# Gate and up rows 4 to 21 by 20 products for 24 in groups of three rows, left sums on GpSimd, results kept in DRAM

## The chip, the cores and the metric

The kernel runs on one core of a Trainium2 chip. The metric is the device time of one execution in microseconds (us). Before the change it is 1108.66 us, the median of 3 runs (1106.58 to 1109.56). Lower is better.

Engines are named as in the profile: PE (TensorE, matrix products), PEld (its weight loads), DVE (VectorE), ACT (ScalarE), POOL (GpSimd) and SP (SyncE, which here only issues transfers). X<-Y means that an instruction writes X from Y.

## The reference

One step of a decoder layer on 544 tokens (512 of a prompt and 32 samples), width 1024, in fp32: half a feed-forward network, a mixer (attention beside an mLSTM), and half a feed-forward network again. The change touches both feed-forward halves alone:

```python
def half_ffn(x, g_pre, g_post, w_gate, w_up, w_down):     # w_gate, w_up: 1024 x 2816; w_down: 2816 x 1024
    h = rmsnorm(x, g_pre)
    u = jax.nn.silu(h @ w_gate) * (h @ w_up)
    return x + 0.5 * rmsnorm(u @ w_down, g_post)
```

## The kernel before

**Split numbers.** Every factor of a product is split into a high part (a cast to fp32r) and a low part (the factor less its high part). A product is three matmuls: high by high, high by low, low by high. `parts` (L240) makes the two: a cast on ACT (L241), then a subtraction on DVE (L242), whose two inputs both lie in SBUF.

**Tiles.** Tokens are columns (544, two halves of 272). 2816 hidden units are 22 rows of 128, and the contraction over 1024 is 8 tiles of 128. One matmul is 128 x 128 by 128 x 272.

**Gate and up rows 0 to 3** (`PLAIN`) are computed plainly (L588 to L595), row by row, by `mm3`. Rows 2 and 3 make eight jobs of 24 matmuls, while the right-hand factors for what follows are begun.

**Gate and up rows 4 to 21** are nine steps of two rows (`quadrants`, L488). A step takes [gate; up] x two halves of the contraction x two halves of the tokens by 7 products in place of 8. Sums of weight blocks (left sums) and sums of token blocks (right sums, made once in `right_parts` and `factors`) feed the products; both are made on DVE (`plus`, L499, and `less`/`neither`, L454/L457). A product is 24 matmuls (`seven`), a step 168. Results come out of PSUM through copies on ACT (L531) and additions on DVE (L499 with a PSUM input), then silu (L535, L541) and a multiplication (L544, L549). Weights of the next step are loaded one step ahead, 1024 KB each for gate and up, on SP's queue. The kept hidden rows 0 to 15 stay in SBUF (`ha`; rows 0 to 3 make a trip through DRAM, `u_keep`), and rows 16 to 21 (`OWN`) are split into high and low parts at once.

**Down** (`down`, L703) begins with a lead: plain products of rows 16 to 21, 12 groups of 18 matmuls, for which only those rows are needed. Under the lead, the first factors of the kept rows 0 to 15 are made (`making`), for 7 products of four quarters each. Weights of the down product come in on SP's queue and are added up by accumulating transfers on POOL's queue (L732).

**The order of work.** Each engine runs its own queue in order. A list scheduler writes the queues from the program: it may move an instruction ahead of others on its engine when it thinks it ready, and a buffer is handed to its next tile when the last reader of the old one is done. Split weights go through `w_tiles` (L244), three buffers of each kind; PSUM has eight banks (`acc` 3, `aux` 3, `smp` 2).

Of the kernel before, what the change touches and what calls it, by code (L numbers as in the profile page):

```python
# [50 lines left out]
PRODUCTS = (1, 5, 6, 2, 7, 3, 4)  # L51
# [138 lines left out]
class _Halves:  # L190
# [4 lines left out]
    def __getitem__(self, key):  # L195
        p, k, *c = key
        if isinstance(k, slice):
            a, b = k.indices(KT)[:2]
            assert a // WK == (b - 1) // WK
            k, i = slice(a % WK, a % WK + b - a), a // WK  # L200
        else:
            k, i = k % WK, k // WK
        return self.tiles[i][(p, k, *c)]


class _Builder:
# [213 lines left out]
    def u_tiles(self, li, ctx):  # L420

        return ctx.enter_context(self.tc.tile_pool(name="u%d" % li, bufs=1))


    def right_parts(self, gi, place, pool):

        nc = self.nc
        n = place[:, 0:KT]

        def scaled(k0):  # L430
            for k in range(k0, k0 + WK):
                nc.vector.scalar_tensor_tensor(out=n[:, k, :], in0=self.X[:, k, :],
                                               scalar=self.minus[:, gi * KT + k:gi * KT + k + 1], in1=self.r,
                                               op0=ALU.mult, op1=ALU.mult)
        scaled(0)
        yield
        h8 = self.h8, "h8"
        places = {p: [(pool, "t")] if p in (1, 5, 6) else [h8] for p in PRODUCTS}
        quarters = [tuple(n[:, k:k + WK, c:c + HALF] for k in (0, WK) for c in (0, HALF))]
        making = self.factors(places, quarters, PRODUCTS)  # L440
        for _ in range(2):
            next(making)
            yield
        scaled(WK)
        yield from making
# [42 lines left out]
    def quadrants(self, loaded, raws, small, kept, put, beside, making):  # L488

        nc = self.nc
        flat = self.X.tiles[0].rearrange("p k t -> p (k t)")
        s3 = flat[:, 0:1024].rearrange("p (k m) -> p k m", k=WK)
        space = flat[:, 1024:1024 + 2 * T].rearrange("p (a t) -> p a t", a=2)
        C0, C1 = slice(0, HALF), slice(HALF, T)

        def plus(out, x, y):
            nc.vector.tensor_tensor(out=out, in0=x, in1=y, op=ALU.add)  # L499
        for u in range(PLAIN, KF, 2):  # L500
            (g0, g1), (u0, u1) = ((r[:, 0:WK], r[:, WK:KT]) for r in loaded)
            if PLAIN < u < KF - 2:
                loaded = raws(u + 2)
            uu = kept(u) if u < KEEP else space
            p1, p5, u2 = (small.tile([128, 2, HALF], F32, name=name) for name in ("p1", "p5", "u2"))
            a, b = [], []
            for p in PRODUCTS:
                if u == PLAIN:
                    next(making, None)
                    if p == 5:  # L510
                        loaded = raws(u + 2)

                if p == 5:
                    plus(s3, g0, u0)
                    plus(u0, u0, u1)
                elif p == 6:
                    plus(u0, u0, g0)
                elif p == 3:
                    plus(u0, u0, g1)
                src = {1: g0, 2: g1, 4: u1, 7: s3}.get(p, u0)  # L520
                w = [x.rearrange("p (k a) m -> p k (a m)", a=2) for x in self.w_tiles()]
                self.parts(src, *w)
                for r in range(2):
                    if p == 1:
                        a.append(self.acc.tile([128, 512], F32, name="acc")[:, 0:HALF])
                    elif p == 5:
                        b.append(self.ps_tile()[:, 0:HALF])
                    ps = b[r] if p in (5, 3) else self.smp.tile([128, 512], F32, name="smp")[:, 0:HALF] if p == 2 else a[r]
                    self.seven(ps, p, w, slice(r * 128, r * 128 + 128), p in (1, 5, 2), p in (2, 3, 4))
                    if p in (1, 5, 6):  # L530
                        nc.scalar.copy(out={1: p1, 5: p5, 6: u2}[p][:, r], in_=ps)  # L531
                    elif p == 2:
                        x = uu[:, r, C0]
                        plus(x, ps, p1[:, r])
                        nc.scalar.activation(out=x, in_=x, func=AF.Silu, scale=-1.0)  # L535
                    elif p == 7:
                        plus(uu[:, r, C1], ps, p5[:, r])
                    elif p == 3:
                        x = u2[:, r]
                        plus(x, ps, x)  # L540
                        nc.scalar.activation(out=x, in_=x, func=AF.Silu, scale=-1.0)  # L541
                    elif p == 4:
                        x = uu[:, r, C0]
                        nc.vector.tensor_tensor(out=x, in0=ps, in1=x, op=ALU.mult)  # L544
                    if u == PLAIN:
                        next(beside, None)
                if p == 3:
                    x = uu[:, :, C1]
                    nc.vector.tensor_tensor(out=x, in0=x, in1=u2, op=ALU.mult)  # L549
            if u >= KEEP:  # L550
                put(u, uu)

    def ffn(self, li, hs, ws, gpre, gpost, finish, before=None, u=None, lead=None, done=None):
# [7 lines left out]
        with ExitStack() as ctx:  # L561
# [3 lines left out]
            spill = tc.dram_tile([128, PLAIN, T], F32, name="u_keep%d" % li)  # L565
# [78 lines left out]
            place = own.tile([128, 2 * OWN, T], F32, name="u")  # L644
            making = self.right_parts(gpre, place, factors)
# [4 lines left out]
            def raws(m):  # L650
                if m == PLAIN:
                    g = place[:, KT:2 * OWN].rearrange("p k t -> p (k t)")[:, 0:2048].rearrange("p (k m) -> p k m", k=KT)
                else:
                    g = self.raw.tile([128, 8, 256], F32, name="raw")
                u = self.X.tiles[1].rearrange("p k t -> p (k t)")[:, 0:2048].rearrange("p (k m) -> p k m", k=KT)
                if (m - PLAIN) % 4 == 0:
                    u = small.tile([128, 8, 256], F32, name="rawx")
                for r, w in zip((g, u), views):
                    nc.sync.dma_start(out=r, in_=w[:, :, m * 128:m * 128 + 256])
                return g, u  # L660


            steps = 3
            jobs = [(f, m, half) for m in range(2, PLAIN) for half in range(2) for f in (gate, upper)]
            ahead, last = 2, len(jobs) - 3
            done, w = 0, None
            for i, (f, m, half) in enumerate(jobs[:last]):
                if i % 4 == 0:
                    w = {gate: weight(), upper: weight()}
                if i == 0:  # L670
                    first = raws(PLAIN)
                f(m, half, w[f])
                upto = max(0, steps * (i + 1 - ahead) // (last - ahead))
                for _ in range(done, upto):
                    next(making)
                done = upto

            def beside():
                for f, m, half in jobs[last:]:
                    f(m, half, w[f])  # L680
                    yield
            ns = []

            def kept(m):
                if not ns:
                    ns.extend(self.ha.tile([128, WK, T], F32, name="ha") for _ in range(KEEP // WK))
                elif m == PLAIN + 2:
                    nc.gpsimd.dma_start(out=ns[0], in_=spill)
                return ns[m // WK][:, m % WK:m % WK + 2, :]

            def put(m, uu):
                i = 2 * (m - KEEP)
                if i == 0:
                    self.own = own.tile([128, 2 * OWN, T], F32R, name="u")
                s = self.own[:, i:i + 4].rearrange("p (a b) t -> p a b t", a=2)
                self.parts(uu, s[:, 0], s[:, 1])
                rows.update({m + a: (s[:, 0, a, :], s[:, 1, a, :]) for a in range(2)})
            self.quadrants(first, raws, small, kept, put, beside(), making)
            more.__exit__(None, None, None)
            self.down(li, ns, rows, factors, ctx.enter_context(tc.tile_pool(name="late%d" % li, bufs=2)), xd, gpost,  # L700
                      finish)

    def down(self, li, ns, rows, factors, late, xd, gpost, finish):  # L703
# [4 lines left out]
        t, h8 = (factors, "t"), (self.h8, "h8")  # L708
# [50 lines left out]
        def close():  # L759
            i, up, hs, w, ps = held.pop(0)  # L760
            for half, p in zip(hs, ps):
                plain(p, w, half, OWN - 2, 2, False, True)
                nc.scalar.activation(out=y[half][:, 4 * up + i, :], in_=p, func=AF.Copy, scale=-1.0 if up else 1.0)
        for i, up, hs in lead:
# [4 lines left out]
            for half, p in zip(hs, ps):  # L769
                plain(p, w, half, 0, OWN - 2, True, False)  # L770
# [1240 lines left out]
```

## Time and profile before

| | before |
|---|---|
| median of 3 runs | 1108.66 us (1106.58 to 1109.56) |
| profiled execution, first to last instruction | 1109.2 us |
| PE busy | 1088.8 us (98%), clock 0.995 |
| DVE busy | 855.4 us (77%) |
| ACT busy | 639.5 us (58%) |
| POOL busy | 163.2 us (15%), most of it issuing transfers |
| HBM | 144 GB/s over the span |

How to read it: a busy time is the time in which an engine had an instruction in execution, of the profiled execution's span. A wait is named after what ended it. The profile gives no time of the execution outside its span; that span lies 0.5 us above the median of the runs.

### The profile page before, as it was taken

The page shows a single profiled execution, that of the slowest core. Times are in us where ns is not written, and L with a number is a line of the kernel's source. Part 1 is how long each engine was busy: PE and PEld are TensorE (multiplying, and loading weights), DVE is VectorE, ACT ScalarE, POOL GpSimd, SP SyncE. Part 2 cuts the span into 40 slices and gives each one's busy share as a digit, 9 for nine tenths or more (in the row PEclk, how much of TensorE's full clock was granted, in tenths as well). Part 3 has the DMA queues.
Part 4 walks back from the last instruction along what each step waited for, and adds up shares of the span by engine and source line. Part 5 has one row for each costly group of instructions (what it writes and reads, how often), then busy time and mean ns, then how long its engine had stood idle before and what let it go on. Part 6 is the DMA issues. An engine that isn't in the chain of part 4 may idle for free. (4 is left out here: it accounts for less than half of the span.)

```text
span 1109.2 us, 21539 instructions
## 1 busy us (share of the span) xinstructions
PE 1088.8 (98%) x8610; PEld 1050.2 (95%) x8610; DVE 855.4 (77%) x1626; ACT 639.5 (58%) x1288; POOL 163.2 (15%) x212
## 2 busy tenths in 40 slices
PE   9999999999999999999999999999999999999997
PEld 8999999999999998899789888999999999999997
DVE  5898787887677898668666477799978778957865
ACT  6554544565567756666545466675555455555664
POOL 3100000001210424320333442001000000012000
PEclk9999999999999999999999999999999999999999
DMA  9723233237994346533345545864223323299832
GB/s 265 252 94 114 81 111 115 76 96 208 223 245 128 93 121 172 175 112 82 103 148 160 178 136 177 248 216 161 89 87 105 114 77 106 67 270 206 191 97 81
DMA packets 145588, 160.33 MB, mean 145 GB/s; under 512 B 6013, under 2 KB 135397, under 8 KB 144208
## 3 DMA queue, kind: packets, MB, share of 16 engines
q1 hardware_dynamic: 115008, 99.05, 29.5%
q0 software_dynamic: 27472, 57.14, 20.8%
q10 hardware_dynamic: 3008, 2.78, 0.9%
q8 instruction: 67, 1.10, 0.4%
q14 instruction: 33, 0.27, 0.1%
HBM read 143.19 MB, written 16.28 MB: 144 GB/s over the span
## 5 line engine op out<-in xcount | busy, mean ns | idle before, releaser
L241 ACT CAST wh<-raw 128x512 fp32r<-128x512 f32 (+2 forms) x165 | 126.8, 795 | 97.3 <-PE acc L254 34.3
L242 DVE TENSOR_TENSOR wl<-raw,wh 128x512 fp32r<-128x512 f32 (+2 forms) x165 | 146.9, 904 | 43.4 <-ACT wh L241 42.7
L253 PE MATMUL acc<-h,wh 128*128 128x272 f32 x552 | 165.7, 300 | 0.0
L255 PE MATMUL acc<-h,wl 128*128 128x272 f32 x552 | 161.4, 293 | 0.0
L254 PE MATMUL acc<-h,wh 128*128 128x272 f32 x552 | 161.0, 292 | 0.0
L483 PE MATMUL acc<-t,wh 128*128 128x272 f32 x472 | 136.7, 290 | 0.0
L485 PE MATMUL acc<-t,wl 128*128 128x272 f32 x472 | 136.5, 290 | 0.0
L484 PE MATMUL acc<-t,wh 128*128 128x272 f32 x472 | 136.1, 289 | 0.0
L253 PEld LDWEIGHTS acc<-h,wh 128*128 128x128 f32 x552 | 104.9, 190 | 8.1 <-issue 7.5
L255 PEld LDWEIGHTS acc<-h,wl 128*128 128x128 f32 x552 | 104.9, 190 | 0.6 <-issue 0.4
L254 PEld LDWEIGHTS acc<-h,wh 128*128 128x128 f32 x552 | 105.1, 190 | 0.3 <-DVE y L1459 0.2
L483 PE MATMUL acc<-h,wh 128*128 128x272 f32 x360 | 104.2, 290 | 0.0
L485 PE MATMUL acc<-h,wl 128*128 128x272 f32 x360 | 104.2, 289 | 0.0
L484 PE MATMUL acc<-h,wh 128*128 128x272 f32 x360 | 103.6, 288 | 0.0
L242 DVE TENSOR_TENSOR wl<-X,wh 128x1024 fp32r<-128x1024 f32 x66 | 80.7, 1223 | 28.3 <-ACT wh L241 28.3
L241 ACT CAST wh<-X 128x1024 fp32r<-128x1024 f32 x66 | 69.3, 1050 | 40.6 <-PE aux L484 26.0
L484 PEld LDWEIGHTS acc<-t,wh 128*128 128x128 f32 x472 | 89.0, 189 | 0.0
L483 PEld LDWEIGHTS acc<-t,wh 128*128 128x128 f32 x472 | 88.8, 188 | 0.0
L485 PEld LDWEIGHTS acc<-t,wl 128*128 128x128 f32 x472 | 88.7, 188 | 0.1
L732 POOL DMA_DIRECT2D late<-in_ffn_w_down_dram x12 | 18.8, 1563 | 439.4 <-DVE wl L242 241.6
L485 PE MATMUL aux<-h,wl 128*128 128x272 f32 x240 | 69.6, 290 | 0.4 <-DVE wl L242 0.4
L483 PE MATMUL aux<-h,wh 128*128 128x272 f32 x240 | 69.4, 289 | 0.0
(522 smaller groups left out, 3288.6 us busy)
## 6 DMA issues: line engine op xcount, KB each, us to landing
raw<-in_ffn_w_gate_dram SPq DMA_DIRECT2D x18, 1024.0 KB, 5.8
raw<-in_w_in_dram SPq DMA_DIRECT2D x28, 512.0 KB, 4.8
late<-in_ffn_w_down_dram POOLq DMA_DIRECT2D x12, 1024.0 KB
rawx<-in_ffn_w_up_dram SPq DMA_DIRECT2D x10, 1024.0 KB
X<-in_ffn_w_up_dram SPq DMA_DIRECT2D x8, 1024.0 KB, 5.4
raw<-in_ffn_w_down_dram SPq DMA_DIRECT2D x8, 1024.0 KB, 8.6
raw<-in_ffn_w_down_dram SPq DMA_DIRECT2D x10, 768.0 KB, 4.5
raw<-in_w_out_dram SPq DMA_DIRECT2D x7, 1024.0 KB, 5.3
```

Source lines behind the costliest of these rows:

```text
L241: self.nc.scalar.copy(out=high, in_=src)
L242: self.nc.vector.tensor_tensor(out=low, in0=src, in1=high.bitcast(F32), op=ALU.subtract)
L253: nc.tensor.matmul(ps, lhsT=wh, rhs=xh(k0 + k), start=st, stop=False)
L254: nc.tensor.matmul(ps, lhsT=wh, rhs=xl(k0 + k), start=False, stop=False)
L255: self.last_mm = nc.tensor.matmul(ps, lhsT=wl, rhs=xh(k0 + k), start=False, stop=sp).ins
L483: nc.tensor.matmul(ps, lhsT=wh[:, k, cs], rhs=high, start=st, stop=False, skip_group_check=True)
L484: nc.tensor.matmul(ps, lhsT=wh[:, k, cs], rhs=low, start=False, stop=False, skip_group_check=True)
L485: self.last_mm = nc.tensor.matmul(ps, lhsT=wl[:, k, cs], rhs=high, start=False, stop=sp, skip_group_check=True).ins
L732: nc.gpsimd.dma_start(out=ts[j], in_=rows_of(a, j, up), accum_op=ALU.add)
```

## The change

Rows 4 to 21 become six groups of three rows (`triples`, in place of `quadrants`). A group takes three rows x four blocks of contraction x two halves of tokens by 20 products in place of 24. A left block is 128 rows of gate and the same of up by two contraction tiles (128 x 512 in SBUF), a right block two contraction tiles by 272 tokens (128 x 544). A product is 12 matmuls, 6 for gate and 6 for up, so a group has 240.

- Left sums (`SUMS`, 16 in a group) run on POOL, in place of DVE, partly in the weight buffers themselves and partly in six scratch pieces s0 to s5 at the ends of these buffers.
- Right factors: 8 scalings on DVE as before, then 20 products' factors of 128 x 544, of which 16 need a sum, on POOL. They lie in the token tiles X0 and X1, which are free by then, and other pools. Two steps of this are taken after each of seven jobs, the rest in the first group. The jobs now all stand before the first group; before, three of them ran beside the first step.
- Every product's 128 x 512 left block is split by ACT and DVE as before; two products share one pair of split buffers.
- Products accumulate in eight chains (`CHAINS`), each with two PSUM banks, four at a time. Nine times in a group a chain's state in between is copied out by ACT for gate and up; seven times DVE adds PSUM to SBUF; seven further sums of 128 x 544 (`both`) run four on POOL and three on DVE.
- Weights are loaded in 8 transfers of 384 KB a group on SP's queue, into eight home buffers: four from `small` and `raw`, four from the kernel's `ha` tiles.
- So hidden rows 4 to 15 are no longer kept in `ha`: each half row is stored to DRAM by SP (136 KB each), and after the last group rows 0 to 15 are loaded back into four `ha` tiles by four transfers of 1088 KB on POOL's queue, where before one such transfer brought back rows 0 to 3. Rows 16 to 21 are split into `t` tiles.

The queues, as built. On POOL, inside rows 4 to 21 (`u`, `ha`, `raw`, `rawx` are home buffers, scratch pieces and places of results), before:

```order
L586 DMA u_keep_410<-sqe 128x272 x4
L688 DMA ha<-u_keep_410 128x2176
L732 DMA late_3000<-in_ffn_w_down_dram 128x8x256
L732 DMA late_3002<-in_ffn_w_down_dram 128x8x256
L732 DMA late_3000<-in_ffn_w_down_dram 128x8x256
```

and now, a third of the way through (L534 a left sum, L549 a sum of results):

```order
L549 TENSOR_TENSOR u_921<-u_921,ha_912 128x544
L549 TENSOR_TENSOR ha_911<-ha_911,u_921 128x544
L534 TENSOR_TENSOR raw_899<-raw_900,rawx2_897 128x512
L534 TENSOR_TENSOR ha_910<-raw_899,raw_900 128x512
L534 TENSOR_TENSOR rawx2_897<-rawx2_897 128x4x128
L534 TENSOR_TENSOR raw_899<-raw_899,rawx2_897 128x512
L534 TENSOR_TENSOR ha_909<-raw_900,raw_899 128x512
L534 TENSOR_TENSOR raw_900<-raw_900 128x4x128
L534 TENSOR_TENSOR rawx0_898<-raw_899,rawx0_898 128x512
L534 TENSOR_TENSOR ha_909<-ha_909 128x4x128
L549 TENSOR_TENSOR u_922<-u_922,ha_912 128x544
L549 TENSOR_TENSOR u_921<-u_921 128x544
```

POOL went from transfers alone to 20 sums a group.

On DVE, in the middle of rows 4 to 21, before (L499 a left sum or an addition out of PSUM):

```order
L499 TENSOR_TENSOR rawx<-rawx,raw 128x1024
L242 TENSOR_TENSOR wl<-rawx,wh 128x1024
L242 TENSOR_TENSOR wl<-raw,wh 128x1024
L499 TENSOR_TENSOR rawx<-rawx,raw 128x1024
L242 TENSOR_TENSOR wl<-X_85,wh 128x1024
L499 TENSOR_TENSOR X_85<-raw,X_86 128x1024
L499 TENSOR_TENSOR X_86<-X_86 128x1024
L499 TENSOR_TENSOR ha<-smp,p_1362 128x272
```

and now (L594 an addition out of PSUM, L792 the multiplication by the gate):

```order
L263 TENSOR_TENSOR wl_1489<-ha_909,wh_1488 128x512
L594 TENSOR_TENSOR ha_912<-acc_1371,ha_912 128x272
L263 TENSOR_TENSOR wl_1489<-ha_911,wh_1488 128x512
L594 TENSOR_TENSOR ha_912<-acc_1372,ha_912 128x272
L263 TENSOR_TENSOR wl_1524<-ha_911,wh_1523 128x512
L263 TENSOR_TENSOR wl_1524<-raw_899,wh_1523 128x512
L263 TENSOR_TENSOR wl_1563<-ha_909,wh_1562 128x512
L549 TENSOR_TENSOR ha_911<-ha_911,u_921 128x544
L263 TENSOR_TENSOR wl_1563<-ha_909,wh_1562 128x512
L594 TENSOR_TENSOR u_922<-aux_1391,ha_911 128x272
L594 TENSOR_TENSOR u_922<-aux_1392,ha_911 128x272
L792 TENSOR_TENSOR u_922<-u_922 128x272
```

The left sums of 128 x 1024 have left this queue; the subtractions are half as long and twice as many for the same weights.

On DVE at the passage to `down`, now (`ha` with 128x4x272 are sums of reloaded rows, raw_3374 the down weights of the lead):

```order
L263 TENSOR_TENSOR wl_3469<-raw_3374,wh_3468 128x768
L263 TENSOR_TENSOR u_3413<-ha_3357,u_3413 128x1088
L263 TENSOR_TENSOR t_3075<-u_922,t_3075 128x272
L496 TENSOR_TENSOR ha_3357<-ha_3357 128x4x272
L496 TENSOR_TENSOR ha_3356<-ha_3358,ha_3356 128x4x272
L496 TENSOR_TENSOR ha_3357<-ha_3359,ha_3357 128x4x272
L263 TENSOR_TENSOR wl_3513<-raw_3374,wh_3512 128x768
```

Before, the rows at this place read tiles that had been in SBUF; now three sums of reloaded tiles (the last two loaded are ha_3358 and ha_3359) stand ahead of the fourth split of the lead's weights.

The diff, cut to its core:

```diff
-PRODUCTS = (1, 5, 6, 2, 7, 3, 4)
+ROWS = 3
+ORDER = (11, 5, 4, 2, 1, 16, 7, 9, 8, 19, 0, 12, 17, 18, 6, 10, 13, 3, 14, 15)
+CHAINS = ((11, 4), (5, 7, 9), (2, 16, 0), (1, 8), (19, 12, 17), (18,), (6, 13, 14), (10, 3, 15))
+RIGHT = {11: ("00", 1, "21"), 5: ("00",), 4: ("00", 1, "31"), 2: ("21",), 1: ("20", -1, "21"), 16: ("10", 1, "21"),
...
+SUMS = {11: ("02=02-22", "s3=00-02"), 5: ("s0=10-13", "s0=s0-s3"), 4: ("10=10-20", "s1=13-10"),
+        2: ("s2=11-12", "s5=s2+s3"), 16: ("s2=s2+22",), 7: ("12=12-22",), 19: ("s4=01-03", "s2=s4-s2"),
+        0: ("s4=21-s4",), 18: ("s1=s1+s4", "s1=23-s1"), 3: ("01=01-21",)}
...
+        for i, p in enumerate(ORDER):
...
+                    nc.gpsimd.tensor_tensor(out=out, in0=x, in1=block(y), op=ALU.add if sign > 0 else ALU.subtract)
+                    x = out
+                self.parts(x, high, low)
+            yield
...
+    def left_sum(self, text, views):
...
+        self.nc.gpsimd.tensor_tensor(out=out, in0=x, in1=y, op=ALU.add if op == "+" else ALU.subtract)
...
+            for s, p in enumerate(ORDER):
+                if i == 0:
+                    next(making, None)
+                for text in SUMS.get(p, ()):
+                    self.left_sum(text, views)
+                if s % 2 == 0:
+                    wh, wl = (x.rearrange("p (b k a m) -> p b k a m", b=2, k=2, a=2) for x in
+                              (y.rearrange("p k m -> p (k m)") for y in self.w_tiles()))
+                self.parts(views[LEFT[p]], wh[:, s % 2], wl[:, s % 2])
...
+                if p == 1:
+                    both(at["8"], at["8"], at["1"], nc.gpsimd)
+                    both(at["11"], at["11"], at["10"], nc.gpsimd)
+                elif p == 16:
+                    both(at["8"], at["8"], at["9"])
...
+                for k in (2, 0, 3, 1):
+                    for a in range(2):
+                        c = (PLAIN + i * ROWS) * 128
+                        nc.sync.dma_start(out=homes[i % 2][k][:, :, a, :], in_=views[a][:, 2 * k:2 * k + 2, c:c + ROWS * 128])
...
+                if i:
+                    _take(making, 2)
...
+                if m < KEEP:
+                    nc.vector.tensor_tensor(out=x, in0=x, in1=g, op=ALU.mult)
+                    nc.sync.dma_start(out=spill[:, m, self.cols(half)], in_=x)
...
+            ns = [self.ha.tile([128, WK, T], F32, name="ha") for _ in range(KEEP // WK)]
+            for i, x in enumerate(ns):
+                nc.gpsimd.dma_start(out=x, in_=spill[:, WK * i:WK * i + WK])
```

More of the change, by code (lines that the diff above doesn't have):

```diff
@@ L203, in __getitem__, with __init__, one @@
         return self.tiles[i][(p, k, *c)]
+class _Pair:
+    def __init__(self, *tiles):
+        self.tiles = tiles
+    def one(self, a):
+        return self.tiles[a] if len(self.tiles) == 2 else self.tiles[0][:, a * HALF:a * HALF + HALF]
 class _Builder:
@@ L642, in ffn @@
             factors = ctx.enter_context(tc.tile_pool(name="t%d" % li, bufs=3))
-            place = own.tile([128, 2 * OWN, T], F32, name="u")
-            making = self.right_parts(gpre, place, factors)
+            making = self.right_parts(gpre, own, factors)
             more = tc.tile_pool(name="more%d" % li, bufs=1)
@@ L648, in ffn @@
             views = self.ffn_views(li)
[L650 to L660, printed above, removed]
@@ new lines, in places @@
+            def places(i):
+                if not spots:
+                    for _ in range(2):
+                        x = generic(own, (WK, T), name="u")
+                        spots.extend(x[:, j * T:j * T + T] for j in range(4))
+                names = ("8", "10", "11", "1", "9", "20", "01", "6", "y")
+                rest = iter(spots)
+                at = {}
+                for name in names:
+                    if name in ("8", "10"):
+                        flat = pieces[4 + 2 + (name == "10")][:, 6 * 256:6 * 256 + T]
+                    elif i == 0 and name in ("11", "1", "9"):
+                        t = "sq" if name == "11" else "sqe"
+                        at[name] = _Pair(*(self.tmp.tile([128, HA], F32, name=t, bufs=3 if t == "sq" else 4) for _ in range(2)))
+                        continue
+                    else:
+                        flat = next(rest)
+                    at[name] = _Pair(flat)
+                at["x"], at["21"] = at["1"], at["9"]
+                return at
@@ L664, in ffn @@
+            spots = []
             jobs = [(f, m, half) for m in range(2, PLAIN) for half in range(2) for f in (gate, upper)]
-            ahead, last = 2, len(jobs) - 3
-            done, w = 0, None
-            for i, (f, m, half) in enumerate(jobs[:last]):
+            w = None
+            for i, (f, m, half) in enumerate(jobs):
                 if i % 4 == 0:
                     w = {gate: weight(), upper: weight()}
-                if i == 0:
-                    first = raws(PLAIN)
                 f(m, half, w[f])
[L673 to L697, printed above, removed]
```

231 lines of the change are left out of this document (150 added, 81 removed), and 3 rows, old and new, of the table RIGHT.

## The prediction

> **What bounds the kernel now.** First the page's busy times, then the stretch that is changed, cut by one step of two rows (columns: busy time and instructions of PE, PEld, DVE, ACT, POOL; clock; DMA share; GB/s), then the durations of single operations.
>
> ```profile
> span 1109.2 us, 21539 instructions
> PE 1088.8 (98%) x8610; PEld 1050.2 (95%) x8610; DVE 855.4 (77%) x1626; ACT 639.5 (58%) x1288; POOL 163.2 (15%) x212
> ...
> 130.40:151.60 21.20, 21.20 (x170) 21.20 (x169) 16.77 (x22) 10.68 (x17) 0.00 (x0) 1.00 0.32 100
> 151.60:172.80 21.20, 21.20 (x170) 21.20 (x169) 16.77 (x22) 10.68 (x17) 0.00 (x0) 1.00 0.32 100
> ```
>
> PE never waits in the stretch: a step of 168 matmuls takes 21.20 us, 0.1262 us a matmul at clock 1.00. DVE has 4.4 us to spare in it, ACT 10.5, and POOL does nothing. So a matmul less is worth 0.126 us, as long as every engine that feeds PE stays below PE's time.
>
> **The change, part by part.**
>
> *Matmuls.* Per network 9 x 168 = 1512 become 6 x 240 = 1440: 72 x 0.1262 = 9.1 us less. A group is 240 x 0.1262 = 30.3 us of PE.
>
> *The work that feeds PE*, from groups that keep shapes apart (the DVE rows of window 40 to 300, ACT and POOL of the whole span):
>
> ```profile
> L242 DVE TENSOR_TENSOR wl<-raw,wh 128x1024 fp32r<-128x1024 f32 x17 | 20.8, 1223 | 3.9 <-ACT wh L241 3.9
> L549 DVE TENSOR_TENSOR ha<-ha,u 128x544 f32<-128x544 f32 x6 | 4.3, 719 | 0.0
> L432 DVE SCALAR_TENSOR_TENSOR u<-X,minus,r 128x544 f32<-128x544 f32 x8 | 6.0, 774 | 0.0
> L585 DVE TENSOR_TENSOR sqe<-sqe,sq 128x272 f32<-128x272 f32 x7 | 2.9, 432 | 0.0
> L499 DVE TENSOR_TENSOR u<-aux,u 128x272 f32<-128x272 f32 x18 | 7.9, 438 | 3.2 <-PE aux L485 3.1
> ...
> L242 DVE TENSOR_TENSOR wl<-raw,wh 128x512 fp32r<-128x512 f32 x88 | 58.2, 685 | 6.1 <-ACT wh L241 5.4
> L241 ACT CAST wh<-raw 128x512 fp32r<-128x512 f32 x88 | 50.2, 618 | 36.1 <-PE acc L254 30.6 <-DMA raw<-in_w_in_dram 2.5 <-DMA out_dram<-y 2.2
> L531 ACT COPY p<-aux 128x272 f32<-128x272 f32 x36 | 13.7, 382 | 3.3 <-PE aux L485 3.3
> L541 ACT ACTIVATE u<-u 128x272 f32<-128x272 f32 x36 | 15.3, 428 | 28.5 <-DVE u L499 28.4
> ...
> L319 POOL TENSOR_TENSOR ssp<-ssp,sq 128x272 f32<-128x272 f32 x7 | 5.4, 768 | 8.9 <-ACT sq L316 8.5
> L1918 POOL TENSOR_TENSOR ha<-ha 16x512 f32<-16x512 f32 x2 | 2.5, 1256 | 48.9 <-ACT ha L1917 48.9
> ```
>
> ACT in a group: 20 casts x 0.618 + 18 copies x 0.382 + 6 silu x 0.428 = 21.8 us of 30.3, hidden.
>
> DVE in a group: 20 subtractions x 0.685 + 3 sums x 0.719 + 6 multiplications x 0.432 = 18.5 us with both inputs in SBUF, and 14 additions out of PSUM x 0.438 = 6.1. Together 24.6 of 30.3: hidden, taken alone.
>
> POOL: 272 columns cost 768 ns and 512 cost 1256, so (1256 - 768)/240 = 2.03 ns a column, and 544 columns 1.32 us by the same line (an estimate; the 512 row has 16 partitions, which I take for the price at 128). A group: 16 left sums x 1.256 + 4 sums x 1.32 = 25.4 us of 30.3. Hidden as well, taken alone.
>
> *DVE and POOL together* is the question. The timeline shows what ran beside each other (columns: start, duration, instruction); then the group of one line of POOL copies:
>
> ```profile
> 17.87 4.99 POOL L319 TENSOR_TENSOR ssp<-ssp,sq 128x272 f32<-128x272 f32 x6 [8.50 <-ACT sq L316]
> 20.60 0.49 DVE L301 SCALAR_TENSOR_TENSOR ha<-aux,gain,ha 128x272 fp32r<-128x272 f32 x1
> ...
> 419.91 0.67 DVE L242 TENSOR_TENSOR wl<-raw,wh 128x512 fp32r<-128x512 f32 x1
> 420.05 0.61 POOL L1782 COPY qz<-X 64x32 f32<-64x32 f32 x1 [4.45 <-DVE X L1225]
> ...
> 680.33 0.43 DVE L1828 TENSOR_TENSOR h<-X,h 128x272 fp32r<-128x272 f32 x1
> 680.52 0.31 POOL L1807 COPY ogs<-q 128x32 f32<-128x32 f32 x1 [1.61 <-ACT q L1660]
> ...
> L1782 POOL COPY qz<-X x8: 204/208/610, 403.0 to 434.9; 64x32 f32<-64x32 f32 x8
> ...
> 627.35 0.21 POOL L1560 COPY cs<-ncol 128x8 f32<-128x8 f32 x1
> 627.41 0.70 DVE L242 TENSOR_TENSOR wl<-raw,wh 128x512 fp32r<-128x512 f32 x1
> ```
>
> The POOL sums that give the price ran beside DVE work that reads PSUM, with one tile in SBUF at most, so they don't show POOL beside a DVE instruction that reads two. The copies do. One that takes 0.21 us took 0.61 when it began 0.14 us into a DVE subtraction of two SBUF tiles, and ended 0.08 us after that one's end (420.58 against 420.66); 0.31 in the second pair, ending 0.07 after. POOL stands still until DVE is through. The other direction has one row, a subtraction of 0.70 us instead of 0.685 over a copy that reads 8 columns: too short to tell. I take it that the two take turns at one resource. The Trainium skill's page "SBUF — State Buffer", section "Who interferes with whom", says that a DVE instruction with two SBUF inputs contends with a GpSimd instruction that reads SBUF, and that whichever starts first keeps the shared port for its whole length. The rows above agree for DVE first; no row shows POOL first.
>
> Taking turns, a group needs the sum of both. Three prices:
> - Bare streams, which is the least. DVE's slope is (1.223 - 0.685)/512 = 1.05 ns a column: 20 x 0.538 + 3 x 0.572 + 6 x 0.286 = 14.2; POOL 16 x 1.041 + 4 x 1.106 = 21.1. Sum 35.3 us.
> - Whole durations, the most: 18.5 + 25.4 = 43.9 us.
> - Streams and 0.08 us of hand-over for each of the 49 instructions, as the copies show it: 35.3 + 3.9 = 39.2 us. I take this one.
>
> All three are above PE's 30.3. Then PE waits for left blocks, in every group: 5.0, 13.6 or 8.9 us. Five groups of a network: 25, 68 or 44.5.
>
> *The first group and the jobs before it.* After the first job 7 jobs x 24 x 0.1262 = 21.2 us and the first group's 30.3 give PE 51.5 us of work. On POOL stand 16 right sums of 544, 16 left sums, 1 sum of 544 and 6 of 272 (some tiles are in halves there). On DVE 8 scalings, 4 weight splits of 1024, 4 multiplications, 20 right and 20 left subtractions, 5 sums and 6 multiplications. By bare streams 38.8 + 35.6 = 74.4 us; by whole durations 47.1 + 45.9 = 93.0; with 0.08 us for each of the 106, 82.9. PE loses 22.9, 41.5 or 31.4 us.
>
> *Results to DRAM and back.* The stores (136 KB each, on SP) are 6 a group beside 3 MB of weights: (3.1 + 0.8) MB in 30 us or more is 130 GB/s at most, below the 209 of the row that follows. Hidden. The reload can't all be early: its last two tiles take the place of weights that the group's last products read, and down's fourth split on DVE stands behind sums that read them. PE has cover then: about four products (6 us) and three lead groups of 36 matmuls (13.6), less some 4 us of DVE and ACT work after landing, 15.5 us. In that time 2.2 MB of reload share the queues with the down weights (X0, X1, late):
>
> ```profile
> 960.00:1005.00 45.00, 44.71 (x356) 44.49 (x354) 29.02 (x34) 23.64 (x38) 4.73 (x3) 1.00 0.83 209
> ```
>
> At that stretch's 209 GB/s the reload alone takes 11 us and lands in time; all four tiles and 2 MB of weights ahead of them take 31 and cost 16. I take 4 us, since half of the reload is issued earlier.
>
> *The sum.* Per network: 44.5 + 31.4 + 4 - 9.1 = 70.8 us. Two networks: +141.6, on the profiled execution's 1109.2: 1251. That execution lies 0.5 above the median, so 1250. Bounds: bare streams and no reload wait, 2 x (25 + 22.9 - 9.1) = +78, 1187; whole durations and the full wait, 2 x (68 + 41.5 + 16 - 9.1) = +233, 1342.
>
> **The rivals.**
>
> *1. The sums hide; faster.* POOL waits only for a DVE instruction already running, and DVE never for POOL. A POOL sum then meets a two-tile DVE instruction 18.5/30.3 = 61% of the time and loses half of one, 0.32 us: 20 x 0.61 x 0.32 = 3.9, so 25.4 + 3.9 = 29.3 us, still under 30.3. It decides where a group's POOL time passes 30.3. Then only the matmuls count, -18.2, and the reload's 4 us twice: 1109.2 - 18.2 + 8 - 0.5 = 1098. For it: every row of before shows POOL waiting, and none DVE. Against: POOL must still read two tiles for 1.04 us in each sum while DVE starts a new instruction every 0.6 us.
>
> *2. The sums hide, the reload doesn't.* As 1, with 16 us lost at each passage to down: 1109.2 - 18.2 + 32 - 0.5 = 1122. For it: DVE's queue has the reloaded tiles' sums ahead of the lead's fourth split. Against: part of the reload leaves early.
>
> *3. Turns in part.* The port is given up between pieces of an instruction, and half of the excess shows: per network (44.5 + 31.4)/2 + 4 - 9.1 = 32.9, two 65.7: 1174. No row speaks for it; the copies waited whole instructions out.
>
> That the change does not do what it says can be left aside: the built PE queue has the 2880 matmuls of the 12 groups.
>
> **How the numbers follow.** The forecast, turns throughout, 0.78; rival 1 0.12; rival 2 0.05; rival 3 0.05. The predicted time is 1250 us, its own range 1187 to 1342. A measurement of this kernel can tell about 0.3% from no change, 1105.3 to 1112.0. Rival 1 is faster unless the reload waits eat it (0.10 of 0.12; the other 0.02 is within the bound); the rest is slower: 0.10, 0.02, 0.88. For 8 in 10 I leave out the top of the forecast's own range above 1320 (0.06) and rival 1 (0.12), and go down to 1115, which takes in rivals 2 and 3: 1115 to 1320.
>
> **What would show it.** In a middle group the time from its first matmul to the next group's first should be 35 to 44 us, with PE idle before its matmuls or weight loads on DVE's `wl` (L263), and DVE on POOL's sums or by itself. The mean of L263 at 128 x 512 should rise from 0.685 towards 1.2 us or more, and L534 on POOL from 1.26 towards 1.7 or more, each where it meets the other; ACT's casts stay at 0.62. If L263 and L534 stay at 0.69 and 1.26 and the groups take 30.3 us, the turns are wrong and rival 1 stands. If L534 alone grows, POOL waits one way. An idle PE at the lead's fourth group with DVE waiting for a transfer from `u_keep` shows the reload. The clock should stay at 1.00 in working stretches; a lower one would be a cost that I have not counted.

## The result, and the profile after

The changed kernel takes 1285.62 us, median of 4 runs (1283.11 to 1287.62), against 1108.6 us before, the median of 4 (1106.58 to 1109.56): a ratio of 1.160, 95% interval 1.157 to 1.163. The forecast was 1250, the direction and the mechanism as forecast, 36 us too low.

The page of the changed kernel, its span and PE's rows:

```profile
span 1284.5 us, 22483 instructions
...
PE 1131.0 (88%) x8466; PEld 1077.6 (84%) x8466; DVE 1051.4 (82%) x1822; ACT 681.6 (53%) x1554; POOL 603.0 (47%) x496
...
PEclk9977988899899999999999999986799888989999
```

PE fell from 98% to 88% busy, and its clock drops below full speed where the change lies. By stretch (columns as in the prediction: length, busy time and instructions of PE, PEld, DVE, ACT, POOL, clock, DMA share, GB/s): the first group, the second group, and the lead of down.

```profile
82.40:138.90 56.50, 40.13 (x240) 38.20 (x241) 52.23 (x54) 23.15 (x51) 46.58 (x34) 0.76 0.29 89
138.98:179.82 40.84, 33.19 (x243) 32.67 (x242) 37.08 (x42) 18.07 (x44) 31.45 (x20) 0.87 0.32 100
336.00:374.00 38.00, 30.84 (x218) 30.09 (x217) 22.85 (x28) 17.83 (x30) 3.02 (x4) 0.87 0.89 256
```

The second group has 40.8 us for a work of PE that I had put at 30.3; DVE is busy for 37.1 of it and POOL for 31.5, where each alone would need 24.6 and 25.4. The lead took 27.7 us before and takes 38.0 now. The rest of the first network's down is 76.4 us in both. The mixer behind it came out 2.8 us shorter in the new trace, which is scatter: from the end of the first lead to the same product of the second network the trace of before took 444.6 us, this one 441.8, and those of the runs below 437.1 to 443.0.

What a single instruction costs now, in groups that keep shapes apart:

```profile
L263 DVE TENSOR_TENSOR wl<-ha,wh 128x512 fp32r<-128x512 f32 x96 | 120.2, 1252 | 0.0
L263 DVE TENSOR_TENSOR wl<-rawx,wh 128x512 fp32r<-128x512 f32 x72 | 92.6, 1295 | 1.5
L594 DVE TENSOR_TENSOR ha<-acc,ha 128x272 f32<-128x272 f32 x48 | 20.6, 428 | 0.0
L549 DVE TENSOR_TENSOR ha<-ha,u 128x544 f32<-128x544 f32 x10 | 15.7, 1574 | 15.2 <-POOL ha L549 15.2
...
L534 POOL TENSOR_TENSOR ha<-ha 128x512 f32<-128x512 f32 x36 | 58.8, 1632 | 1.0
L549 POOL TENSOR_TENSOR u<-u,ha 128x544 f32<-128x544 f32 x22 | 39.0, 1775 | 8.0 <-DVE u L594 8.0
...
L262 ACT CAST wh<-ha 128x512 fp32r<-128x512 f32 x96 | 58.6, 624 | 11.6 <-PE acc L584 7.8 <-PE smp L584 2.4 <-POOL ha L534 1.1
```

The subtraction that took 0.685 us averages 1.25 to 1.30; a DVE sum of 544 columns went from 0.72 to 1.57. A left sum on POOL, 1.256 by the row of before, takes 1.63 in the largest group and 1.59 on average over all 192. The DVE additions that read one tile from PSUM stayed at 0.43, ACT's casts at 0.62. So of the work of these three engines what grew is DVE's instructions with two SBUF inputs, and POOL's sums.

The timeline inside the second group (start, duration, instruction; DVE's rows, then POOL's, then one each of ACT and PE):

```profile
149.21 1.43 DVE L263 TENSOR_TENSOR wl<-ha,wh 128x512 fp32r<-128x512 f32 x1
150.56 1.79 DVE L263 TENSOR_TENSOR wl<-raw,wh 128x512 fp32r<-128x512 f32 x1
152.27 1.78 DVE L263 TENSOR_TENSOR wl<-ha,wh 128x512 fp32r<-128x512 f32 x1
...
159.95 0.43 DVE L594 TENSOR_TENSOR u<-aux,ha 128x272 f32<-128x272 f32 x1
...
148.47 1.62 POOL L534 TENSOR_TENSOR ha<-ha 128x512 f32<-128x512 f32 x1
150.16 1.64 POOL L534 TENSOR_TENSOR rawx<-rawx,ha 128x512 f32<-128x512 f32 x1
151.88 1.62 POOL L534 TENSOR_TENSOR rawx<-ha,rawx 128x512 f32<-128x512 f32 x1
...
160.41 0.43 ACT L563 ACTIVATE u<-u 128x272 f32<-128x272 f32 x1 [8.87 <-DVE u L594]
...
162.78 0.59 PE L582 MATMUL acc<-h,wh 128*128 128x272 f32 x1 [7.03 <-ACT u L590]
```

DVE and POOL march in step, each with a new instruction 1.71 or 1.72 us after the last (150.56 to 152.27; 150.16 to 151.88). A subtraction's stream (0.54), a sum's (1.04) and two hand-overs of 0.08 make 1.74, so neither overlaps the other. The last two rows show how that reaches PE: DVE's addition at 159.95 is late, the silu that needs it has stood at the head of ACT's queue for 8.87 us, the copies that empty PSUM banks stand behind the silu, and PE waits 7.03 us for a bank. The waits of PE over the whole span (in total, times, longest) name the same place:

```profile
PE acc L582 <- ACT u L590: 60.3, 20, 7.2
...
PE smp L586 <- DVE wl L263: 9.5, 4, 4.2
PE aux L855 <- ACT t L262: 8.6, 2, 4.6
```

### The profile page after: what moved, and what is told of

Read it like the earlier page. It is cut to its first block, busy times and chain, and to the rows that moved or that the text cites. A ratio compares the mean times of both kernels' runs of the same rounds, so it can differ in the third digit from the quotient of the medians.

```text
span 1284.5 us, 22483 instructions
## 1 busy us (share of the span) xinstructions
PE 1131.0 (88%) x8466; PEld 1077.6 (84%) x8466; DVE 1051.4 (82%) x1822; ACT 681.6 (53%) x1554; POOL 603.0 (47%) x496
## 5 line engine op out<-in xcount | busy, mean ns | idle before, releaser
L263 DVE TENSOR_TENSOR wl<-raw,wh 128x512 fp32r<-128x512 f32 (+2 forms) x205 | 209.7, 1036 | 30.6 <-ACT wh L262 29.8
L274 PE MATMUL acc<-h,wh 128*128 128x272 f32 x552 | 164.7, 299 | 0.0
L275 PE MATMUL acc<-h,wh 128*128 128x272 f32 x552 | 159.8, 290 | 0.0
L263 DVE TENSOR_TENSOR wl<-ha,wh 128x512 fp32r<-128x512 f32 (+1 forms) x100 | 124.0, 1240 | 2.4 <-ACT wh L262 2.4
L582 PE MATMUL acc<-h,wh 128*128 128x272 f32 x192 | 66.0, 344 | 53.3 <-ACT u L590 53.3
L274 PEld LDWEIGHTS acc<-h,wh 128*128 128x128 f32 x552 | 104.0, 188 | 8.1 <-issue 7.5
L275 PEld LDWEIGHTS acc<-h,wh 128*128 128x128 f32 x552 | 104.1, 189 | 0.3 <-DVE y L1569 0.2
L263 DVE TENSOR_TENSOR wl<-rawx,wh 128x512 fp32r<-128x512 f32 x72 | 92.6, 1295 | 1.5
L582 PEld LDWEIGHTS acc<-h,wh 128*128 128x128 f32 x192 | 45.2, 235 | 56.2 <-ACT u L590 56.1
L262 ACT CAST wh<-ha 128x512 fp32r<-128x512 f32 (+1 forms) x100 | 61.9, 632 | 12.7 <-PE acc L584 7.8
L274 PE MATMUL acc<-ha,wh 128*128 128x272 f32 x192 | 60.0, 312 | 9.8 <-DVE sq L636 6.1
L276 PE MATMUL acc<-ha,wl 128*128 128x272 f32 x192 | 59.6, 311 | 7.1 <-DVE wl L263 7.1
L584 PE MATMUL acc<-h,wh 128*128 128x272 f32 x192 | 63.6, 331 | 0.0
L534 POOL TENSOR_TENSOR ha<-ha 128x512 f32<-128x512 f32 x36 | 58.8, 1632 | 1.0
L275 PE MATMUL acc<-ha,wh 128*128 128x272 f32 x192 | 58.9, 307 | 0.0
L525 PE MATMUL acc<-u,wh 128*128 128x272 f32 x184 | 53.5, 291 | 0.0
```

The source lines that it names most:

```text
L262: self.nc.scalar.copy(out=high, in_=src)
L263: self.nc.vector.tensor_tensor(out=low, in0=src, in1=high.bitcast(F32), op=ALU.subtract)
L274: nc.tensor.matmul(ps, lhsT=wh, rhs=xh(k0 + k), start=st, stop=False)
L275: nc.tensor.matmul(ps, lhsT=wh, rhs=xl(k0 + k), start=False, stop=False)
L276: self.last_mm = nc.tensor.matmul(ps, lhsT=wl, rhs=xh(k0 + k), start=False, stop=sp).ins
L525: nc.tensor.matmul(ps, lhsT=wh[:, k, cs], rhs=high, start=st, stop=False, skip_group_check=True)
```

## The experiments

The theory is the prediction's: a DVE instruction with two SBUF inputs and a POOL sum take turns, both ways. The rivals were POOL's length by itself, a one-way wait, a longer chain of sums, and any activity of POOL.

### All left sums back on DVE

```diff
     def left_sum(self, text, views):
...
-        self.nc.gpsimd.tensor_tensor(out=out, in0=x, in1=y, op=ALU.add if op == "+" else ALU.subtract)
+        self.nc.vector.tensor_tensor(out=out, in0=x, in1=y, op=ALU.add if op == "+" else ALU.subtract)
```

> The changed kernel with its 16 left sums a group on DVE in place of GpSimd; the sums of results and of right blocks stay on GpSimd. Theory (DVE and GpSimd take turns): GpSimd's sums leave the port, but DVE now has 24.6 + 16 x 0.685 = 35.6 us of work a group, so a middle group takes about 36 us in place of 40.9, L263 at 128x512 comes back to 0.69 to 0.8 us, and the kernel takes about 1230 us (1205 to 1245). Rival (a chain of PSUM copies and additions sets the group, not the port): groups stay near 41 us and the time near 1285.

Measured: 1230.19 us (1229.54 to 1230.83), ratio 1.107 (1.104 to 1.111). A middle group, then a DVE group and a POOL group of this kernel:

```profile
120.83:156.11 35.28, 31.92 (x241) 30.42 (x242) 35.28 (x61) 19.48 (x44) 8.17 (x4) 1.00 0.42 133
```
```profile
L263 DVE TENSOR_TENSOR wl<-ha,wh 128x512 fp32r<-128x512 f32 x96 | 72.1, 761 | 0.2
...
L549 POOL TENSOR_TENSOR u<-u,ha 128x544 f32<-128x544 f32 x22 | 52.3, 2379 | 182.9 <-DVE u L594 102.1 <-ACT u L590 66.7 <-DVE wl L263 14.0
```

DVE, with 16 sums more in its queue, is done sooner than when POOL had them: the second to fifth groups take 34.6 to 37.5 us in place of 40.1 to 41.6. In the group shown DVE is now busy without a gap, which is why the groups are still longer than PE's 29.96. Part of the gain is lost further on: the last groups take 39.3 and 38.8 us in place of 33.8 and 33.5, the leads 41.4 and 41.3 in place of 38.0. The four POOL sums left take 2.38 us at 544 columns when they meet a DVE queue that never pauses.

### POOL writes, but does not read

```diff
-        self.nc.gpsimd.tensor_tensor(out=out, in0=x, in1=y, op=ALU.add if op == "+" else ALU.subtract)
+        for _ in range(2):
+            self.nc.gpsimd.memset(out, 0.5)
```

and the same for POOL's right sums and sums of results.

> The changed kernel with each sum on GpSimd (left, right and of results) replaced by two memsets of the same tile, so GpSimd writes as much and is about as long busy (2 x 0.54 us for 512 columns) but reads nothing; the sums are left out. Theory (turns for SBUF reads): L263 at 128x512 is back at 0.69 us, a middle group takes PE's 30.3 us, and the time is about 1110 us (1098 to 1130), the passage to down still some 10 us late twice. Rival (the chain through PSUM copies sets the group, or the order of the queues does): groups of 38 to 41 us, 1250 to 1285.

Measured: 1106.67 us (1105.39 to 1110.14), ratio 0.9965 (0.9945 to 0.9984). A middle group and the lead; then two groups:

```profile
96.46:126.42 29.96, 29.96 (x243) 29.96 (x242) 21.97 (x44) 19.33 (x44) 19.54 (x40) 1.00 0.43 134
246.20:286.80 40.60, 30.05 (x218) 29.52 (x217) 20.81 (x24) 17.01 (x28) 0.00 (x0) 0.83 0.87 243
```
```profile
L263 DVE TENSOR_TENSOR wl<-ha,wh 128x512 fp32r<-128x512 f32 x96 | 65.9, 686 | 38.6 <-ACT wh L262 38.5
...
L536 POOL MEMSET rawx<- 128x512 f32 x156 | 79.6, 530 | 29.9 <-DVE wl L263 17.8 <-DMA rawx<-in_ffn_w_up_dram 10.4 <-POOLq L2112 0.3
```

All groups take 29.96 us (30.2 the first of the second network) with PE busy throughout, and the subtraction is back at 0.686. The loss in the jobs is gone as well: from 46.0 us to the end of the first group, at 96.4, PE is busy without a gap. So the whole loss up to the lead hangs on POOL's sums. The memsets differ from them in more than the reading: they need no input, and they keep POOL busy for 19.5 us a group, less than the 25.4 of the sums alone. The control further down separates these. This is also the floor of the change: were its sums free, it would gain 0.4%, because the leads still take 40.6 and 38.0 us, 24 us more than before over both networks.

### No reload

```diff
-            for i, x in enumerate(ns):
-                nc.gpsimd.dma_start(out=x, in_=spill[:, WK * i:WK * i + WK])
+            for x in ns:
+                nc.gpsimd.memset(x, 0.5)
```

> The changed kernel without the four transfers that bring rows 0 to 15 back: the four tiles are filled by a memset on GpSimd, which waits for the same buffers to come free; the rows' values are left out. Theory (the reload is late at the lead): the lead takes 28 us in place of 38 in both networks, time about 1265 us (1262 to 1270). Rival (the lead is late for DVE and ACT work left over from the last group, or for a lower PE clock): the lead stays at 36 to 38 us and the time at 1280 to 1286.

Measured: 1269.81 us (1269.37 to 1270.24), ratio 1.143 (1.140 to 1.146). The lead:

```profile
335.90:365.30 29.40, 27.42 (x218) 27.18 (x217) 22.21 (x28) 17.77 (x30) 2.64 (x2) 1.00 0.86 215
```

The leads take 29.4 and 30.2 us in place of 38.0 and 38.0, the groups are as they were. So the reload costs 8.6 and 7.8 us of the 10.3 and 10.9 that the leads have lost; with it, 3.4 us of the 8.6 are matmuls at a lower clock (PE busy for 30.84 against 27.42 over the same 218).

### The kernel before with 12 POOL sums a step

```diff
+            for _ in range(12 if u < KEEP else 0):
+                nc.gpsimd.tensor_tensor(out=extra, in0=uu[:, 0, 0:512], in1=uu[:, 1, 0:512], op=ALU.add)
             if u >= KEEP:
                 put(u, uu)
```

> The kernel before with 12 extra sums of 128x512 on GpSimd after each of the six steps of rows 4 to 15, which read the step's results and write a tile that nobody reads. DVE's queue is unchanged and nothing waits for them. Theory (turns both ways): DVE has 11 instructions of 1024 columns with two SBUF inputs and one of 544 a step, 12.4 us of streams, 13.4 with hand-overs; 12 sums take 12 x 1.12 = 13.4 more, 26.9 us in place of 21.2 in six steps of two networks: about +68 us, 1177 (1140 to 1190), L242 and L499 longer. Rival (GpSimd waits for DVE, never DVE for GpSimd): 1109 us, the sums longer than 1.26 us and L242 at 1.22.

Measured: 1183.72 us (1182.90 to 1184.53), ratio 1.066 (1.062 to 1.069). The timeline of DVE, and the group of the sums:

```profile
152.41 2.32 DVE L242 TENSOR_TENSOR wl<-X,wh 128x1024 fp32r<-128x1024 f32 x1
154.76 2.20 DVE L500 TENSOR_TENSOR X<-raw,rawx 128x1024 f32<-128x1024 f32 x1
157.00 2.19 DVE L500 TENSOR_TENSOR rawx<-rawx 128x1024 f32<-128x1024 f32 x1
159.11 0.43 DVE L500 TENSOR_TENSOR ha<-smp,p 128x272 f32<-128x272 f32 x1
```
```profile
L552 POOL TENSOR_TENSOR extra<-ha 128x512 f32<-128x512 f32 x144 | 301.2, 2092 | 48.4 <-DVE ha L545 38.0
```

Nobody uses these sums, and DVE's queue is the one of before; yet its 1.22 us instructions take 2.2 to 2.3, and the stretch of quadrants 223.0 us (222.1 in the second network) in place of 185.9. This is the direction that no row of before showed: DVE waits for POOL, at almost a whole sum's stream each time (1.0 to 1.1 us). The one-way rival falls.

### The control: POOL as busy, reading one column

```diff
+            for _ in range(12 if u < KEEP else 0):
+                nc.gpsimd.tensor_copy(out=extra[:, 0:1], in_=uu[:, 1, 271:272])
+                nc.gpsimd.memset(extra, 0.5)
+                nc.gpsimd.memset(extra, 0.5)
```

> The control of the run with 12 sums: the kernel before, and after each of the six steps 12 times a GpSimd copy of one column and two memsets of 128x512, which keep GpSimd busy for about as long as the 12 sums but read next to nothing. Turns between two readers of SBUF: writing alone takes no turn, the stretch of quadrants stays at 186 to 190 us and the time at 1109 to 1115; DVE's 128x1024 subtraction stays at 1.22 us. Rival, any busy GpSimd slows DVE (or its writes do): as with the 12 sums, stretch about 222 us, time about 1180, that subtraction about 1.5 us.

Measured: 1108.89 us (1107.49 to 1110.20), ratio 0.9975 (0.9951 to 0.9999); the stretch is 185.9 us as before. Groups of this kernel, and two copies from its timeline:

```profile
L242 DVE TENSOR_TENSOR wl<-X,wh 128x1024 fp32r<-128x1024 f32 x66 | 80.7, 1222 | 29.7 <-ACT wh L241 29.6
...
L552 POOL COPY extra<-ha 128x1 f32<-128x1 f32 x144 | 77.0, 535 | 33.7 <-DVE ha L545 25.0
L554 POOL MEMSET extra<- 128x512 f32 x144 | 75.9, 527 | 8.3
...
136.36 1.07 POOL L552 COPY extra<-ha 128x1 f32<-128x1 f32 x1
...
141.97 0.18 POOL L552 COPY extra<-ha 128x1 f32<-128x1 f32 x1
```

POOL is busy here for 19.0 us of a step of 21.2, more than the 15.1 that 12 sums take by themselves, and writing costs nobody anything: the subtraction stays at 1.222, the memset at 0.525 to 0.533. The copy of one column takes 0.18 us at 141.97, where DVE reads PSUM, and 1.07 at 136.36, behind a sum that DVE had begun at 136.16. The Trainium skill's page "SBUF — State Buffer", section "Who interferes with whom", says that a two-input DVE instruction contends with a GpSimd instruction that reads SBUF and not with one that only writes; this pair of runs agrees (1.52 to 1.60 us on average for DVE's 1024-column subtractions in the run with the sums, 1.22 in this one).

### Half the sums: 6 a step

```diff
+            for _ in range(6 if u < KEEP else 0):
+                nc.gpsimd.tensor_tensor(out=extra, in0=uu[:, 0, 0:512], in1=uu[:, 1, 0:512], op=ALU.add)
```

> The kernel before with 6 additional GpSimd sums (128x512, results used by nobody) after each of the six steps of rows 4 to 15, half of the 12 that took the stretch of quadrants from 185.9 to 222.5 us. Turns at one resource: a step then needs 13.4 us of DVE's two-tile work and 6 x (1.04 + 0.08) = 6.7 us of POOL's, 20.1 us, just below PE's 21.2, so most of it is hidden: the stretch 186 to 195 us, the time 1109 to 1127, about 1115. Rival, each POOL sum costs the kernel the same whatever the total (half of what 12 cost): stretch 204 us, time about 1147. Rival, POOL waits one way: 1109.

Measured: 1142.50 us (1142.27 to 1142.72), ratio 1.030 (1.027 to 1.033); the stretch is 202.0 us (203.8 in the second network). My figure was 1109 to 1127; the rival's 1147 is nearer. POOL's and DVE's timeline, and PE's waits:

```profile
137.86 13.49 POOL L552 TENSOR_TENSOR extra<-ha 128x512 f32<-128x512 f32 x6 [10.41 <-DVE ha L545]
...
141.17 2.32 DVE L242 TENSOR_TENSOR wl<-raw,wh 128x1024 fp32r<-128x1024 f32 x1
```
```profile
PE aux L485 <- DVE wl L242: 26.0, 12, 2.4
```

The total of 20.1 us of two-tile work in a step of 21.2 was no guide. The six sums run in one piece of 13.5 us, in which DVE makes the weight splits and sums that PE needs next. Five of DVE's instructions there (not six, as the next expectation says) take 1.0 to 1.1 us longer; DVE falls 5.2 us behind, and PE runs out of splits once a step, for 2.4 us at the longest.

### The 6 sums, and 12, spread over the step

```diff
                 self.parts(src, *w)
+                if u < KEEP and p != 4:
+                    nc.gpsimd.tensor_copy(out=extra[:, 0:1], in_=w[1][:, 3, 255:256])
+                    nc.gpsimd.tensor_tensor(out=extra, in0=extra, in1=extra, op=ALU.add)
```

> The kernel before with 6 dead-end GpSimd sums (128x512) a step as in the run with 6 in a row (stretch 202.0 us, ratio 1.030), but one behind each of the first six weight splits of the step, held back by a copy of one column of that split. The six in a row lengthened six neighbouring DVE instructions by 1.0 us each and PE ran out of splits there. Theory, the place decides: spread out, each sum costs DVE at most 1.05 us at 3 us distance, 6.3 us a step at most, of which DVE's idle time (4.4 us of 21.2) and its additions from PSUM (3.5 us) take a part; stretch 186 to 194 us, time 1109 to 1126, about 1115. Rival, the total decides (each sum costs PE 0.45 us wherever it stands): stretch 200 to 204 us, time 1137 to 1147.

Measured: 1117.34 us (1114.74 to 1119.94) beside 1105.94 of before in the same comparison, ratio 1.011 (1.004 to 1.018); the stretches are 190.9 and 189.8 us.

> The same with two sums behind each of the first six splits, 12 a step (differences in place of sums, same cost). As 12 in a row they took the stretch from 185.9 to 222.5 us. DVE's two-tile work and POOL's then add up to 26.9 us of 21.2, so the place should matter little: stretch 205 to 225 us, time 1148 to 1188, about 1175. Rival, spreading hides these too: stretch under 195 us, time under 1128.

Measured: 1156.50 us (1155.87 to 1157.13), ratio 1.047 (1.042 to 1.051), stretches 210.5 and 209.1 us. PE's waits with 6, the group of the sums, and one sum from the timeline:

```profile
PE aux L485 <- DVE wl L242: 2.5, 3, 2.0
```
```profile
L527 POOL TENSOR_TENSOR extra<-extra 128x512 f32<-128x512 f32 x72 | 116.7, 1621 | 5.8
...
136.26 1.04 POOL L527 TENSOR_TENSOR extra<-extra 128x512 f32<-128x512 f32 x1
```

Six sums spread out cost 4 to 5 us a stretch instead of 16, and PE's waits for splits fall from 26.0 to 2.5 us. So the place matters as long as the total has room; 12 cost 24 spread and 37 in a row, so there the total decides first. One thing was not kept equal: these sums read the same tile twice and take 1.04 us when nothing meets them (the last row), less than the 1.256 of the sum that gave the price, and they lengthen a DVE instruction by 0.84 us at most, where those in a row did so by 1.10. For the five instructions that were lengthened in each of six steps that is 5 x 6 x 0.26 = 7.8 us at most (an estimate) of the 11 to 14 us a stretch between the two runs with 6, so the place accounts for at least 3; its exact share is not shown. Both fell inside what was expected.

### Half of the left sums on DVE

```diff
-                    self.left_sum(text, views)
+                    self.left_sum(text, views, nc.vector if s < 4 else nc.gpsimd)
```

> The changed kernel with the left sums of each group's first four products on DVE (8 of 16) and the other 8 on GpSimd. Turns: a group's two-tile work is 14.2 + 8 x 0.538 = 18.5 us on DVE and 8 x 1.041 + 4 x 1.106 = 12.8 on POOL, with 0.08 for each of 49 instructions 35.2 us, and DVE alone needs 30.1; middle groups 35 to 38.5 us (the upper end is midway between all sums on DVE and all on GpSimd as measured), the time 1225 to 1257: no split brings the group to PE's 30. Rival, each engine was overloaded by itself, and a split relieves both (DVE 30.1, POOL 8 x 1.26 + 4 x 1.32 = 15.4, both under 30.3): groups about 31 us, time about 1130 to 1140.

Measured: 1264.85 us (1264.14 to 1265.57), ratio 1.141 (1.137 to 1.144); the third to fifth groups take 39.1 to 40.7 us, the second 45.6 and the last 32.5. The middle groups are worse than expected (35 to 38.5), and far from the 31 us of the rival. A POOL group of the first network:

```profile
L534 POOL TENSOR_TENSOR raw<-ha,raw 128x512 f32<-128x512 f32 x6 | 13.6, 2272 | 28.8 <-DVE wl L263 28.8
```

With the sums on both engines, sums in place wait for the other engine's reading of the same block: 28.8 us of POOL's idle time stand before this one sum of each group. That comes on top of the turns; how much of the time it makes was not separated.

No version that does all the work beats the kernel before; with POOL's sums replaced by memsets the changed kernel is 0.4% ahead, and that one leaves the sums out.

## Why the prediction was right, and where it was wrong

Working with the first network (the second in brackets), where a group without contention is 29.96 us:

| term, us per network | forecast | measured |
|---|---|---|
| matmuls | -9.1 | -11.1 (-11.1) |
| five groups | +44.5 | +47.3 (+48.0) |
| jobs and first group | +31.4 | +42.6 (+41.5) |
| passage to down | +4 | +10.3 (+10.9) |
| sum | +70.8 | +89.1 (+89.3) |

The measured matmul term is 1440 x 0.1248 less 1512 x 0.1262; the five groups are 197.1 us (197.8) less 5 x 29.96; the passage is the lead's growth; the jobs and first group are what is left of the stretch up to the lead, +78.8 (+78.4, counted from the same product of the second network on as above). The two sums make 178.4; the spans differ by 175.3, since the mixer between them was 2.8 us shorter.

**The turns** were right, and shown in both directions: by the step of 1.71 us in the changed kernel, by the dead-end sums, and by the control. L263 rose to 1.25 to 1.30 us as said (1.2 or more); L534 to 1.59 on average, short of the 1.7. PSUM additions and casts did not grow, as forecast.

**The middle groups**: 40.9 us against 39.2, between the bounds of 35.3 and 43.9. The five together are 197.1 against 196, and that they agree so well is partly luck: the second to fifth take 163.2 us where 156.8 were forecast, and the last takes 33.8, 5.4 less than forecast, with only four left sums on POOL in it. The sum over the two-tile work, streams and 0.08 us of hand-over each, was near the right price. Counted after the fact, DVE's own 24.6 us plus POOL's streams and hand-overs (21.1 + 1.6), less the 6.1 us of PSUM additions during which POOL runs freely, give 41.2. With all left sums on DVE the four sums left on POOL need 4.7 us, which fit into the 6.1, so that DVE's own 35.6 us are what counts, against 34.6 to 37.5 measured in the second to fifth groups.

**The jobs and the first group** is the term that was mis-sized most: 42.6 (41.5) against 31.4, at the upper bound of 41.5 and a little over. The step that failed counted the 16 left sums of the first group. POOL's left sums by stretch, up to the first group's start, in it, in the second, in the last:

```profile
0.00:82.40 82.40, 11.64 (x8) 0.94 0.60 186
82.40:138.90 56.50, 33.85 (x21) 0.76 0.29 89
138.90:179.80 40.90, 25.08 (x16) 0.87 0.32 100
302.10:336.00 33.90, 6.32 (x4) 1.00 0.53 162
```

29 are done before the second group begins, 13 of them for the second. At 1.04 + 0.08 us each they add 14.6 us, 46.0 for the term. A later part of it comes back in the last group, which has 12 fewer. The count is shown; that it is the cause of the missing 11 us is argued, since no run held POOL back. The other candidate is the clock: the 240 matmuls of the first group took PE 40.1 us in place of 29.96. But DVE is busy for 52.2 of that group's 56.5 us (its row stands with the result), which leaves 4.3 us at most for what a slower PE could have held up there.

**The passage**: 10.3 (10.9) against 4, inside the bounds of 0 and 16. The reload is the cause of 8.6 (7.8), by the run without it. I took a quarter of the worst case because half of the reload leaves earlier; and I looked at DVE's queue, where the trace shows ACT's as the first to stand: its casts of reloaded tiles waited 18.6 us in four waits for the transfer, and PE's wait at the lead ends with an ACT cast (8.6 us, above). The remaining 2 to 3 us are open; in the runs on the kernel before, the leads scatter from 27.1 to 29.1 us.

**How the loss shows**: I expected PE to wait for DVE's `wl`; most of its waiting was for PSUM banks, 60.3 us, behind a silu that waited for DVE. The engine that sets the pace was named rightly, the path from it to PE was not.

**The clock** was named as a cost not counted. It fell to 0.938 over the span, and to 0.76 in the first group. In the lead it is 3.4 us, inside the 8.6 above; in the groups, where PE waits anyway, what it costs was not separated.

**The rivals**: the one-way wait (1098, 1122) falls with the 12 dead-end sums, turns in part (1174) with the step of 1.71 us. Rival 1's own test, POOL's time in a group against PE's, would have been too mild even so: the run with 6 sums shows that work which fits on average still costs where it stands in one piece.

## What to carry to other kernels

Before moving work from DVE to POOL, count DVE instructions with two SBUF inputs beside POOL instructions that read SBUF as one queue: the moved sum costs DVE its stream (1.0 to 1.1 us at 512 columns in the runs) where on DVE it would have cost 0.685, so the move pays only as far as POOL's sums fall where DVE stands still or reads PSUM. A total that fits in PE's time is not enough: look at where the moved work stands, since a piece of 13 us in the wrong place cost 2.7 us a step, and spread out, with somewhat cheaper sums, 0.7 to 0.8. And a result sent to DRAM comes back on the queues that the next stage's weights use: 8 us at each passage here.

## What the runs showed of the hardware that was not expected

- The clock: PE's granted clock was 1.00 where PE was busy for 29.96 of 29.96 us, 0.87 where it was busy for 33.2 of 40.8, and 0.76 for 40.1 of 56.5. Short waits alone did not lower it: in the group shown of the run with all left sums on DVE PE was busy for 31.9 of 35.3 us, with no wait over 1.3, at 1.00. The Trainium skill's page "TensorE: Matmul & The Clock Gate", section "Part 1: The HAM clock gate (the "warmup" mystery)", says that the clock follows how busy PE has been of late; the first three rows agree.
- A matmul of the new groups takes 29.96/240 = 0.1248 us where the old steps had 21.20/168 = 0.1262; no run looked for the cause.
- A POOL copy of a single column, 0.18 us by itself, takes 1.07 us in the row above, behind one 1024-column DVE instruction, and 1.24 at the most: the price of a turn is the other's remaining length, however little is read.
